# Split weights moved 16 bytes into their buffers in a two-layer hybrid decoder trunk

## The chip, the core and the metric

The kernel runs on one NeuronCore of one Trainium2 chip. Its time is device microseconds from start to end of one execution; the time before is the median of 3 runs. TensorE (PE in the rows) multiplies, PEld is its loading of weights, VectorE is DVE, ScalarE is ACT, GpSimd is POOL, and SyncE (SP) issues most DMAs. SBUF is the memory on the chip, 128 partitions of bytes; an address below is a byte offset within a partition. PSUM is where TensorE accumulates.

## What is computed

Two layers over 512 tokens of width 1024, in float32. Each layer is an input projection that feeds four groups of heads (forgetting attention, gated linear attention, latent attention, state-space scan), an output projection, and a gated feed-forward part of width 2816:

```
h = rmsnorm(x, norm1[l])
(fq, fk, fv, ff, gq, ..., sz, sxbc, sdt) = split_cols(h @ w_in[l], IN_SPLITS)
y_a, y_b, y_c, y_d = fox(...), gla(...), mla(...), mamba2(...)
x = x + concatenate([y_a, y_b, y_c, y_d], axis=-1) @ w_out[l]
h2 = rmsnorm(x, norm2[l])
x = x + (silu(h2 @ w_gate[l]) * (h2 @ w_up[l])) @ w_down[l]
...
return rmsnorm(x, final_norm)
```

## The kernel before

Activations lie with features on the partitions and the 512 tokens along them, as tiles of 128 x 512 float32 (2048 bytes a partition). Every large product is done in float32r, a format with fewer bits that TensorE multiplies in one pass, and float32's accuracy is won back by splitting: each operand is a high part (rounded to float32r) and a low part (what the rounding left). One product of 128 features is therefore three matmuls, in `prod` (lines 315 to 317): high weights by high activations, low weights by high activations, high weights by low activations. Each matmul has a weight load of 128 x 128 ahead of it, then streams 512 tokens. `prod_tok` (lines 324 to 326) has the roles exchanged: 128 tokens of an activation are loaded, and 256 columns of a weight are streamed. Attention scores, transposes and the small products of the scans are plain float32 matmuls, except the forgetting attention's scores (line 692).

Weights come in 204 units of at most 128 x 1024. The class `Weights` holds them: `load` (line 282) issues a DMA into one of two raw buffers `wr`; `split` makes the high part `wh` on ACT (line 293) and the low part `wl` on DVE (line 294), each in one of three buffers; `get` hands out the next unit and keeps two ahead. One unit serves 24 matmuls of 512 columns in the gate, up and front products, and 21 or 24 in the down products.

Order of the work: the front of a layer (normalised activations `n_0h`, `n_0l`, products named `ft`, `sm`, `fkp`, `fqp`, `mckv`, `mcq`, `gq`, `gk`), the heads, whose generators a `Runner` steps between the projections, the output products (`oa`, `og`, `om`), and then the feed-forward part in three pieces of 8, 7 and 7 hidden blocks: for each block a gate product `g` and an up product `u` (activations from the pool `act`), an activation, and the split of the result into `uh` and `ul` (pool `mix`); after each piece eight down products `d` (`dl` in the last piece, whose last two output blocks go in halves of 256 tokens).

Where things lie. Each pool is a run of SBUF addresses, in the order in which the pools are made: constants, residual, `act` (normalised activations), `weights`, `small`, `mix`. The first tile of `small` is a pad of `PAD` float32 that nothing uses; it moves all of `small` and `mix`. In the built program of before:

| buffers | first address | modulo 64 |
|---|---|---|
| `act`: high parts, low parts | 30432, 46816 | 32, 32 |
| `wr` | 63200 | 32 |
| `wh`, `wl` | 71392, 83680 | 32, 32 |
| `uh`, `ul` and all else in `mix` | from 104672 | 32 |

Tiles are multiples of 64 bytes long and blocks start at multiples of 512 bytes, so every float32r product of lines 315 to 326 has both operands at 32 modulo 64: they lie at 0 from each other. The exceptions are constants (`ident`, `ones`, `sel`: 0).

`joint_gates` (line 419 on) computes the gates of two head groups in small tiles of 128 x 32 on DVE; each of its values has a tile of its own.

Of the kernel before, what the change touches and what calls it, by code (L numbers as in the profile page):

```python
# [19 lines left out]
F32R = mybir.dt.float32r  # L20
# [3 lines left out]
P = 128  # L24
# [14 lines left out]
RAWS, PARTS = 2, 3  # L39
# [2 lines left out]
WARM = 14  # L42
ROPE_AT = 3
SECOND_HALF = 4
PAD = 72


FIRST = """N0 A0 P00 N1 A1 P10 P01 P11 N2 P02 P12 B0 N3 P03 P13 B1 N4 P04 P14 N5 P05 P15 N6 P06 P16 N7 P07 P17 W2 Q0 Q1 Q2 Q3
# [87 lines left out]
def trunk(tc, I, out, shapes, depth=2):  # L136
# [3 lines left out]
    def blk(i, n=P):  # L140
        return slice(i * n, (i + 1) * n)

    from contextlib import ExitStack
    with ExitStack() as es:
# [4 lines left out]
        wp = pool("weights", bufs=3)  # L149
        sp = pool("small", bufs=1)  # L150
        mp = pool("mix", bufs=1)

        sp.tile([P, PAD], F32, tag="pad", name="pad")
        pj = pool("psum_proj", bufs=2, space=PSUM)
# [6 lines left out]
        def ps_mix(name):  # L161
            return pm.tile([P, T], F32, tag="pm", name=name)
# [4 lines left out]
        def tmp(tag, name, cols=T, dt=F32, parts=P):  # L167
            return mp.tile([parts, cols], dt, tag=tag, bufs=RINGS[tag], name=name)
# [74 lines left out]
        cs = cp.tile([P, T], F32, name="cs")  # L243
# [26 lines left out]
        class Weights:  # L270
# [14 lines left out]
            def split(self, pieces=1):  # L285

                if not self.loaded:
                    list(self.load())
                raw, i, nk, ncol = self.loaded.pop(0)
                n = nk * ncol  # L290
                h, lo = (wp.tile([P, 1024], F32R, tag=f"w{c}", bufs=PARTS, name=f"w{c}{i}") for c in "hl")
                for c in (blk(j, n // pieces) for j in range(pieces)):
                    S.copy(h[:, c], raw[:, c])  # L293
                    V.tensor_tensor(lo[:, c], raw[:, c], h.bitcast(F32)[:, c], op=ALU.subtract)  # L294
                    yield h, lo
                self.ready.append(tuple(t[:, :n].rearrange("p (k c) -> p k c", k=nk) for t in (h, lo)))
# [55 lines left out]
        class Norm:  # L352
# [43 lines left out]
            def first_two(self, pa_, pb_, split=KC - 1, with_col=True):  # L396

                wa, wb = W.get(), W.get()
                for ks in (range(split), range(split, KC)):
                    for ps, w in ((pa_, wa), (pb_, wb)):  # L400
                        last = prod(ps, w, self.act, ks=ks)
                with tc.issue_after(last.ins):
                    if with_col:
                        self.columns()
                        return self.spread()
                    ps = ps_mix(f"{self.name}ms")
                    PE.matmul(ps, lhsT=ones, rhs=self.acc, start=True, stop=True)
                    return rsqrt(ps, D, "f", self.name, sp.tile([P, T], F32, tag="rn", name=f"{self.name}r"))
# [13 lines left out]
        def joint_gates(l, sm, res):  # L422

            ps = ps_mix(f"jg{l}")
            for b in range(NB):
                PE.transpose(ps[:, 8 * b:8 * b + 8], sm[0:8, blk(b)], ident[0:8, 0:8])
            j = lambda nm: sp.tile([P, 4, 8], F32, tag=f"j{nm}", name=f"j{nm}{l}")
            f2 = lambda t: t.rearrange("p b c -> p (b c)")
            bcast = lambda t: t.unsqueeze(1).broadcast_to((P, 4, 8))
            y, e, s, s2, p, spl, a, csum, tot = (j(n) for n in ("y", "e", "s", "q", "p", "sp", "a", "cs", "tot"))  # L430
            V.tensor_tensor(y, ps[:, 0:32].rearrange("p (b c) -> p b c", b=4), bcast(gsgn), op=ALU.mult)
            V.tensor_tensor(y, y, bcast(gbias[:, l, :]), op=ALU.add)
            V.scalar_tensor_tensor(e, y, -1.0, y, op0=ALU.mult, op1=ALU.max)
            S.activation(e, e, AF.Exp, scale=-1.0)

            V.tensor_scalar(s, e, 2.0, None, op0=ALU.add)
            V.reciprocal(s, s)
            V.tensor_tensor(s, e, s, op=ALU.mult)
            V.tensor_tensor(s2, s, s, op=ALU.mult)
            V.tensor_scalar(p, s2, 2.0 / 17, None, op0=ALU.mult)  # L440
            for k in range(7, 0, -1):
                V.scalar_tensor_tensor(p, p, 2.0 / (2 * k + 1), s2, op0=ALU.add, op1=ALU.mult)
            V.scalar_tensor_tensor(p, p, 2.0, s, op0=ALU.add, op1=ALU.mult)
            V.scalar_tensor_tensor(spl, y, 0.0, p, op0=ALU.max, op1=ALU.add)
            V.tensor_tensor(a, spl, bcast(gfac[:, l, :]), op=ALU.mult)
            yield
            pc_ = ps_mix(f"jc{l}")
            PE.matmul(pc_[:, 0:32], lhsT=tri, rhs=f2(a), start=True, stop=True)
            PE.matmul(pc_[:, 32:64], lhsT=ones, rhs=f2(a), start=True, stop=True)
            V.tensor_copy(f2(csum), pc_[:, 0:32])  # L450
            V.tensor_copy(f2(tot), pc_[:, 32:64])

            pre = sp.tile([P, 3, 4], F32, tag="jpre", name=f"jpre{l}")
            V.tensor_copy(pre[:, 0, :], tot[:, 0, 0:4])
            for b in (1, 2):
                V.tensor_tensor(pre[:, b, :], pre[:, b - 1, :], tot[:, b, 0:4], op=ALU.add)
            V.tensor_tensor(csum[:, 1:4, 0:4], csum[:, 1:4, 0:4], pre, op=ALU.add)
            yield
            pr = ps_mix(f"jr{l}")
            for b in range(NB):  # L460
                PE.transpose(pr[0:8, blk(b)], csum[:, b, :], ident)
            rows = sm[0:8]
            S.copy(rows, pr[0:8, :])
            rr = sp.tile([40, T], F32R, tag="jrr", name=f"jrr{l}")
            G.memset(rr.bitcast(F32), 0.0)
            V.tensor_copy(rr[0:8], rows)
            V.tensor_tensor(rr[32:40], rows, rr.bitcast(F32)[0:8], op=ALU.subtract)

            ncs = sp.tile([P, 4, 4], F32, tag="jn", name=f"jn{l}")
            V.tensor_scalar(ncs, csum[:, :, 4:8], -1.0, None, op0=ALU.mult)  # L470
            dec = sp.tile([P, 4, 4], F32, tag="jd", name=f"jd{l}")
            V.tensor_tensor(dec, ncs, tot[:, :, 4:8], op=ALU.add)
            res.update(rr=rr, spl=spl, ncs=ncs, dec=dec, tot=tot)
# [414 lines left out]
        for l in range(depth):  # L888
# [8 lines left out]
            V.tensor_tensor(sm, ps, r, op=ALU.mult)  # L897
            gates = {}
            R.start(joint_gates(l, sm, gates))


            rg, fr = [], []
            for j in range(10):
# [5 lines left out]
                a = tmp("f", f"fa{l}_{j}")  # L909
# [5 lines left out]
                else:  # L915
                    c = tmp("f", f"cv{l}_{j}")
# [52 lines left out]
            for c in range(2):  # L969
                hold = {}  # L970
                for nm, scale, one, row in (("k", 1.0, -1.0, 66), ("q", -0.125, 1.0, 64)):
                    ps = ps_proj(f"f{nm}p{l}_{c}")
                    prod(ps, W.get(), act)
                    for hh in range(2):
                        h, sl = 2 * c + hh, blk(hh, 64)
                        t = tmp("f", f"f{nm}t{l}_{h}", parts=64)
                        a, b = (tmp("cb"[c], f"f{nm}{i}{l}_{h}", dt=F32R, parts=n) for i, n in (("a", P), ("b", 68)))
                        V.scalar_tensor_tensor(t, ps[sl], scale, r[sl], op0=ALU.mult, op1=ALU.mult)
                        S.copy(a[0:64], t)
                        lo, again = (b[0:64], a[64:128]) if nm == "k" else (a[64:128], b[0:64])  # L980
# [72 lines left out]
            for i in range(4):  # L1053
                w = W.get()
# [8 lines left out]
            for nm, ops in (("g", mix_g), ("m", mix_m)):  # L1063
                if nm == "m":
                    R.drain(g_m)
                for i in range(2):
                    w = W.get()
# [15 lines left out]
            for j0, j1 in HID_PARTS:  # L1083
                us = []
                for j in range(j0, j1):
# [5 lines left out]
                    t, s = tmp("f", f"ft{l}_{j}"), tmp("f", f"fs{l}_{j}")  # L1091
# [48 lines left out]
```

## Time and profile before

| | |
|---|---|
| median of 3 runs | 1269.92 us (1268.7 to 1270.27) |
| profiled execution | 1269.87 us |
| its span, first to last instruction | 1268.1 us |
| granted TensorE clock, mean | 0.994 |
| PE busy | 1248.9 us (98%) |
| DVE busy, ACT busy | 694.0 us (55%), 533.5 us (42%) |

A matmul's end is modelled in this profile, and one matmul's record runs on into the next one's, so TensorE's pace is read from the starts of matmuls that follow one another, not from their durations. In rows of single instructions the first column is the start in microseconds, the second the duration. A granted clock of 1.00 is TensorE's level of 2.4 GHz, 0.50 the level of 1.2 GHz.

### The profile page before, as it was taken

How to read it: one execution, taken by the hardware profiler on the slowest of the kernel's cores; microseconds unless marked ns; L12 is line 12 of the kernel's file. 1: busy time of each engine (PE TensorE's matmuls, PEld its weight loads, DVE VectorE, ACT ScalarE, POOL GpSimd, SP SyncE). 2: the span in 40 equal slices, each digit the busy share in tenths (PEclk: the TensorE clock that was granted, in tenths of full speed). 3: DMA queues.
4: the chain of work that ended last, by engine and by line, in shares of the span. 5: the costliest groups of instructions: out<-in, count | busy, mean ns of one | idle time of the engine just before them, and what ended most of it. 6: DMA issues, size and time to landing. Idle time of an engine off the chain costs nothing.

```text
span 1268.1 us, 16210 instructions
## 1 busy us (share of the span) xinstructions
PE 1248.9 (98%) x6402; PEld 1014.5 (80%) x6402; DVE 694.0 (55%) x1132; ACT 533.5 (42%) x882; POOL 179.1 (14%) x163
## 2 busy tenths in 40 slices
PE   9999999989999999999999999999899999999997
PEld 7887787768888888888888877777788888888886
DVE  7877697565443333344557677966644334433444
ACT  6557765543222222223444577565422222212232
POOL 0103210031100110111301122000211011101111
PEclk9999999989999999999999999999999999999999
DMA  6222121113333333332323221212233223333232
GB/s 206 89 84 67 58 68 45 47 60 116 90 95 99 100 94 91 103 96 89 110 83 101 84 67 43 67 34 67 68 116 97 89 96 100 89 109 98 88 89 76
DMA packets 32907, 109.99 MB, mean 87 GB/s; under 512 B 4096, under 2 KB 4256, under 8 KB 32832
## 3 DMA queue, kind: packets, MB, share of 16 engines
q1 hardware_dynamic: 31968, 108.54, 27.7%
q8 instruction: 50, 0.82, 0.3%
q10 hardware_dynamic: 288, 0.34, 0.1%
q14 instruction: 25, 0.20, 0.0%
q0 software_dynamic: 576, 0.08, 0.0%
HBM read 106.79 MB, written 2.10 MB: 86 GB/s over the span
## 4 chain that ended last, share of the span: by engine, by line
PE 92%; DVE 5%; ACT 2%; DMA 1%; issue 0%; POOL 0%; SPq 0%; DVEq 0%
PE u L315 6%; PE u L316 6%; PE u L317 6%; PE g L317 6%; PE g L315 6%; PE g L316 6%; PE d L315 5%; PE d L316 5%; PE d L317 5%; PE ft L317 3%; PE ft L316 3%; PE ft L315 3%; PE sm L692 1%; PE oa L316 1%; PE oa L315 1%; PE oa L317 1%
## 5 line engine op out<-in xcount | busy, mean ns | idle before, releaser
L293 ACT CAST wh<-wr 128x1024 fp32r<-128x1024 f32 (+2 forms) x206 | 210.3, 1023 | 567.1 <-issue 342.5
L294 DVE TENSOR_TENSOR wl<-wr,wh 128x1024 fp32r<-128x1024 f32 (+2 forms) x206 | 249.9, 1213 | 73.2 <-ACT wh L293 73.0
L315 PE MATMUL d<-uh,wh 128*128 128x512 f32 x296 | 115.1, 389 | 0.0
L316 PE MATMUL d<-uh,wl 128*128 128x512 f32 x296 | 115.1, 389 | 0.0
L317 PE MATMUL d<-ul,wh 128*128 128x512 f32 x296 | 115.1, 389 | 0.0
L1097 DVE TENSOR_TENSOR ft<-u,fs 128x512 f32<-128x512 f32 x44 | 30.4, 692 | 132.7 <-PE u L317 127.1
L1111 DVE TENSOR_TENSOR xT<-xT,d 128x512 f32<-128x512 f32 x40 | 27.5, 688 | 104.6 <-PE d L317 104.6
L1094 POOL TENSOR_TENSOR fs<-fs,n_0r 128x512 f32<-128x512 f32 x22 | 38.3, 1744 | 280.4 <-ACT fs L1093 280.4
L1094 POOL TENSOR_TENSOR fs<-fs,n_1r 128x512 f32<-128x512 f32 x22 | 38.3, 1745 | 279.3 <-ACT fs L1093 279.3
L317 PE MATMUL g<-n_1l,wh 128*128 128x512 f32 x176 | 69.0, 392 | 2.3 <-DVE n_1l L364 2.3
L317 PE MATMUL g<-n_0l,wh 128*128 128x512 f32 x176 | 69.0, 392 | 2.3 <-DVE n_0l L364 2.3
L315 PE MATMUL g<-n_0h,wh 128*128 128x512 f32 x176 | 69.0, 392 | 0.8 <-ACT n_0h L363 0.8
L315 PE MATMUL g<-n_1h,wh 128*128 128x512 f32 x176 | 69.0, 392 | 0.8 <-ACT n_1h L363 0.8
L315 PE MATMUL u<-n_0h,wh 128*128 128x512 f32 x176 | 69.5, 395 | 0.0
L316 PE MATMUL u<-n_0h,wl 128*128 128x512 f32 x176 | 69.4, 394 | 0.0
L317 PE MATMUL u<-n_0l,wh 128*128 128x512 f32 x176 | 69.4, 394 | 0.0
L315 PE MATMUL u<-n_1h,wh 128*128 128x512 f32 x176 | 69.0, 392 | 0.0
L317 PE MATMUL u<-n_1l,wh 128*128 128x512 f32 x176 | 69.0, 392 | 0.0
L316 PE MATMUL u<-n_1h,wl 128*128 128x512 f32 x176 | 68.9, 392 | 0.0
L316 PE MATMUL g<-n_0h,wl 128*128 128x512 f32 x176 | 68.5, 389 | 0.0
L316 PE MATMUL g<-n_1h,wl 128*128 128x512 f32 x176 | 68.5, 389 | 0.0
L317 PEld LDWEIGHTS d<-ul,wh 128*128 128x128 f32 x296 | 55.6, 188 | 11.6
(614 smaller groups left out, 2823.5 us busy)
## 6 DMA issues: line engine op xcount, KB each, us to landing
wr<-in_weights_dram SPq DMA_DIRECT2D x168, 512.0 KB, 3.5
wr<-in_weights_dram SPq DMA_DIRECT2D x32, 448.0 KB, 3.2
xT<-in_x_dram SPq DMA_DIRECT2D x8, 256.0 KB, 6.8
out_dram<-foo SPq DMA_DIRECT2D x8, 256.0 KB, 2.4
wr<-in_weights_dram SPq DMA_DIRECT2D x6, 256.0 KB, 4.1
posi<-in_positions_dram ACTq DMA_DIRECT2D x1, 256.0 KB, 3.0
fkb<-jrr POOLq DMA_DIRECT2D x8, 4.0 KB, 2.7
fqb<-jrr POOLq DMA_DIRECT2D x8, 4.0 KB, 1.7
```

The lines of the kernel that those rows point to most:

```text
L293: S.copy(h[:, c], raw[:, c])
L294: V.tensor_tensor(lo[:, c], raw[:, c], h.bitcast(F32)[:, c], op=ALU.subtract)
L315: PE.matmul(ps, lhsT=wh[:, k, c0:c0 + P], rhs=ah, start=k == 0, stop=False)
L316: PE.matmul(ps, lhsT=wl[:, k, c0:c0 + P], rhs=ah, start=False, stop=False)
L317: last = PE.matmul(ps, lhsT=wh[:, k, c0:c0 + P], rhs=al, start=False, stop=k == n - 1)
L692: PE.matmul(ps[:, :n], lhsT=q[:d, blk(qb)], rhs=k[:d, :n], start=i == 0, stop=i == len(terms[h]) - 1)
L1094: G.tensor_tensor(s, s, r, op=ALU.mult)
L1097: V.tensor_tensor(t, pu, s, op=ALU.mult)
L1111: V.tensor_tensor(xT[m], xT[m], ps, op=ALU.add)
```

## The change

`wh` and `wl` get 1040 columns in place of 1024 (4160 bytes a partition), and what is used of them begins at column 4, 16 bytes in. To make room, `PAD` goes from 72 to 16, and in `joint_gates` the values `a` and `csum` take over the tiles of `e` and `s`, which have been read for the last time by then. In the built program the split weights then lie at 48 modulo 64 (first used byte 71408), `act` stays at 32, and `uh`, `ul` and the rest of `mix` move to 0. Modulo 64 bytes the operands of the gate, up and front products lie at 48 from the weights (32 - 48), and those of the down products at 16 (0 - 48). Output products of the heads and of the latents read one kind or the other: `oa`, `og`, `om` operands are in `act`, the latents' in `mix`. No instruction is added, removed or moved on any engine; the waits are the same ones, and the tile names `ja` and `jcs` are gone.

```diff
-PAD = 72
+PAD = 16
...
-                h, lo = (wp.tile([P, 1024], F32R, tag=f"w{c}", bufs=PARTS, name=f"w{c}{i}") for c in "hl")
+
+                h, lo = (wp.tile([P, 1040], F32R, tag=f"w{c}", bufs=PARTS, name=f"w{c}{i}")[:, 4:1028] for c in "hl")
                 for c in (blk(j, n // pieces) for j in range(pieces)):
                     S.copy(h[:, c], raw[:, c])
                     V.tensor_tensor(lo[:, c], raw[:, c], h.bitcast(F32)[:, c], op=ALU.subtract)
...
-            y, e, s, s2, p, spl, a, csum, tot = (j(n) for n in ("y", "e", "s", "q", "p", "sp", "a", "cs", "tot"))
+            y, e, s, s2, p, spl, tot = (j(n) for n in ("y", "e", "s", "q", "p", "sp", "tot"))
+            a, csum = e, s
```

## Rows read from the trace of the kernel before

**Rows 1.** The page: engines' busy time, share of span, instructions; then the chain by engine.
```profile
PE 1248.9 (98%) x6402; PEld 1014.5 (80%) x6402; DVE 694.0 (55%) x1132; ACT 533.5 (42%) x882; POOL 179.1 (14%) x163
...
PE 92%; DVE 5%; ACT 2%; DMA 1%; issue 0%; POOL 0%; SPq 0%; DVEq 0%
```

**Rows 2.** Busy time by stretch: a warming stretch, then feed-forward parts of both layers.
```profile
core 0: us, PE busy (x) PEld busy (x) DVE busy (x) ACT busy (x) POOL busy (x), PEclk, DMA share, GB/s
273.00:283.00 10.00, 8.84 (x27) 7.06 (x28) 2.37 (x3) 0.26 (x2) 0.56 (x1) 0.66 0.18 54
300.00:360.00 60.00, 60.00 (x267) 49.67 (x266) 24.11 (x27) 17.37 (x22) 10.81 (x6) 1.00 0.32 102
1000.00:1060.00 60.00, 60.00 (x266) 49.69 (x265) 22.35 (x25) 14.36 (x17) 5.40 (x3) 1.00 0.30 97
```

**Rows 3.** Timeline, down products of layer 1: matmuls and the loads beside them.
```profile
999.72 0.39 PE L317 MATMUL d<-ul,wh 128*128 128x512 f32 x1
999.95 0.39 PE L315 MATMUL d<-uh,wh 128*128 128x512 f32 x1
999.95 0.19 PEld L316 LDWEIGHTS d<-uh,wl 128*128 128x128 f32 x1
1000.17 0.39 PE L316 MATMUL d<-uh,wl 128*128 128x512 f32 x1
1000.18 0.19 PEld L317 LDWEIGHTS d<-ul,wh 128*128 128x128 f32 x1
...
1011.96 0.39 PE L317 MATMUL d<-ul,wh 128*128 128x512 f32 x1
```

**Rows 4.** Timeline, token products of layer 0, 256 columns: first and last of 38.
```profile
86.83 0.28 PE L325 MATMUL fvp<-wl,n_0h 128*128 128x256 f32 x1
...
91.27 0.28 PE L326 MATMUL fvp<-wh,n_0l 128*128 128x256 f32 x1
```

**Rows 5.** Timeline: plain float32 scores of 512 columns, and what follows them.
```profile
216.63 1.88 PE L692 MATMUL sm<-mkh,mqh 128*128 128x512 f32 x4
218.34 0.60 PE L709 MATMUL ptm<-ident,asm 128*128 128x128 f32 x4
```

**Rows 6.** Timeline, up products at the lower clock: first and last of nine.
```profile
275.18 0.63 PE L316 MATMUL u<-n_0h,wl 128*128 128x512 f32 x1
...
278.59 0.63 PE L315 MATMUL u<-n_0h,wh 128*128 128x512 f32 x1
```

**Rows 7.** Timeline, output products just after small products of the attention: second of nine on.
```profile
220.93 0.40 PE L316 MATMUL oa<-ms_1mh,wl 128*128 128x512 f32 x1
221.16 0.40 PE L317 MATMUL oa<-ms_1ml,wh 128*128 128x512 f32 x1
...
222.55 0.40 PE L317 MATMUL oa<-f_1ml,wh 128*128 128x512 f32 x1
222.79 0.61 PE L692 MATMUL sm<-mkh,mqh 128*128 128x128 f32 x4
```

**Rows 8.** By tile, durations min/median/max: down products, then some output products.
```profile
L315 PE MATMUL d<-uh,wh x296: 389/389/389, 360.4 to 1140.0; 128*128 128x512 f32 x148
...
L316 PE MATMUL oa<-f_0mh,wl x16: 387/396/504, 195.7 to 860.8; 128*128 128x512 f32 x16
```

**Rows 9.** By line over the span (PE, PEld): line 315, line 324; then `dl`'s shapes.
```profile
0.00:1268.10 1268.10, 605.84 (x1538) 290.01 (x1538) 0.99 0.28 87
...
0.00:1268.10 1268.10, 39.60 (x136) 25.99 (x136) 0.99 0.28 87
...
L315 PE MATMUL dl<-uh,wh x70: 277/389/481, 1216.9 to 1258.4; 128*128 128x512 f32 x42, 128*128 128x256 f32 x28
```

**Rows 10.** Groups by shape: splits of whole units on DVE and ACT; busy, mean, idle before.
```profile
L294 DVE TENSOR_TENSOR wl<-wr,wh 128x1024 fp32r<-128x1024 f32 x168 | 210.8, 1255 | 65.0 <-ACT wh L293 64.8
L293 ACT CAST wh<-wr 128x1024 fp32r<-128x1024 f32 x168 | 176.3, 1052 | 452.6 <-issue 259.2 <-PE d L317 83.7 <-PE g L317 46.0
```

**Rows 11.** By tile: `joint_gates`' `ja`, the value that takes over the tile of `e`.
```profile
L445 DVE TENSOR_TENSOR ja<-jsp,gfac x2: 181/187/193, 38.9 to 660.5; 128x32 f32<-128x32 f32 x2
```

## The prediction

> **What bounds the kernel now.** I read the page first, for who is busy and what the end hangs on: TensorE is busy 98% of the span and makes up 92% of the chain that ended last, DVE 5% [rows 1]. Then the busy time by stretch: in the feed-forward parts TensorE has no idle time at a granted clock of 1.00, the 2.4 GHz level, while DVE is busy 22 to 24 us of 60, ACT 14 to 17, and the DMA share is 0.30 to 0.32 [rows 2]. So no wait is to be looked for; the kernel goes as fast as matmul follows matmul. The third view is the timeline, of which the reader takes starts alone. From 999.72 to 1011.96 us there are 54 gaps between down products, 12.24 / 54 = 226.7 ns each [rows 3]. At 2.4 GHz that is 544 cycles for 512 columns: 32 cycles, 13.3 ns, more than one column a cycle. The token products have 37 gaps in 4.44 us, 120.0 ns or 288 cycles for 256 columns [rows 4]: 32 over again. The excess goes with each load and matmul, not with the columns.
>
> Where does it not appear? Plain float32 scores take 1.71 us for four passes of 512 columns, 427.5 ns each, against 426.7 for a column every second cycle: 0.8 ns over, with the same kind of load beside each [rows 5]. And while the clock stood at its lower level (granted 0.66 on average over that stretch) the same float32r products had 8 gaps in 3.41 us, 426.3 ns, which is 512 columns at 1.2 GHz and nothing over [rows 2, 6]. A fixed price for changing weights would show there too. The load of the next weights begins with the stream, within 10 ns [rows 3], so I read the 13.3 ns as the two disturbing each other in SBUF when the stream takes a column every cycle. The last view says that this depends on how the two lie to each other: right after small products the same shape runs from 220.93 to 222.79 us in 8 gaps, 232.5 ns each [rows 7], and over the run the modelled records of output products have a median of 396 ns and a smallest of 387, where all 296 down products of one line have 389 [rows 8]. In an undisturbed stream it settles at one value.
>
> **The change part by part.** The same instructions stand in the same order. What changes is where loads and streams begin within 64 bytes. Before, they begin 0 apart, in the same 16 bytes; after, one quarter of 64 bytes apart in one direction (48) or the other (16).
>
> 1. The products. 1538 matmuls on each of lines 315 to 317 and 136 on each of 324 to 326 [rows 9]: 3 x 1538 + 3 x 136 = 5022 that load one of the split pair and stream the other. The trace has no products at 16 or 48, so the price per product is bounded from both sides. Best: the excess shrinks to that of the float32 passes, 13.3 - 0.8 = 12.5 ns less, 5022 x 12.5 = 62.8 us. Worst: the gap stays at what the disturbed records show, 396 against 389 ns, 7 ns more, or 35 us. The smallest record, 387, would be 2 ns less, or 10 us. I take half of the excess, 6.7 ns (16 cycles), 5022 x 6.7 = 33.5 us less. It is nearer to the float32 end than to the smallest record, because every row that I have is at offset 0, where both begin in the same place, and that is the one arrangement that the change leaves; and because the settled excess is the same whole 32 cycles in two shapes, I expect another step of the same kind, not a few cycles. The part of the products that run at the lower clock is too small to take off.
>
> A rule of the Trainium skill goes against this: "TensorE: Matmul & The Clock Gate", Step-by-step: what each phase is for, says that TensorE reads SBUF for the stream and for the loads through two independent ports, so that the next load takes nothing from the running matmul. By that rule there would be nothing to win, and the sum would be 0. The same page, Back-to-back issue gap, gives N / 2.4 + 2.5 ns for a single stream, 215.8 ns for 512 columns; this trace disagrees by 10.9 ns a product [rows 3], and if that were the gap after, my estimate from the page would be 1215 us.
>
> 2. The splits. ACT and DVE now write 16 bytes into the buffer, 1052 and 1255 ns for a whole unit [rows 10]. The cover in the feed-forward part is an engine with over half of its time free [rows 2]. Without cover, DVE's 5% of the chain is 63 us [rows 1]; if all of it were 5% slower or faster, 3 us either way. I take 0. Faster products ask for a unit every 24 x 220 = 5.3 us where it was 5.4; one split of 1.3 us and one cast of 1.1 fit.
>
> 3. `mix` moves to 0 modulo 64. The attention's own matmuls have both operands in `mix`, which stay 0 apart; constants (`ident`, `ones`) now lie with them where they were 32 away. 6402 - 5022 = 1380 matmul records are left [rows 1, 9]; most are short float32 passes, which have shown 0.8 ns of excess [rows 5]. At that size 1 us either way; I take 0.
>
> 4. `a` and `csum` in the tiles of `e` and `s`: written by DVE after DVE's own last reading of them, two instructions of 187 ns a layer [rows 11], with no new engine to wait for. In layer 1 `e` is written 600 us after layer 0's last reader. 0, and at worst 2 x 0.2 us.
>
> Sum, against the profiled execution: 1269.87 - 33.5 = 1236.4 us. Its span is 1268.1 with 1.8 us around it; the median of the runs differs by 0.05 us, so the same number stands for the median.
>
> **The rivals.**
>
> *No change.* The 32 cycles are the price of changing weights in a one-pass product, or collisions whose number does not depend on where the two begin. For it: 32 cycles for both widths, and a settled gap that holds to the nanosecond through whatever DVE and ACT do [rows 3, 4, 8]. Against it: nothing over at the lower clock, and the wide spread when disturbed [rows 6, 7]. 1269.9, within 2 us.
>
> *Slower: offset 0 is a good place.* The settled gap before lies near the short end of what the disturbed records show (387 to 396 and more). If at 16 and 48 the streams settle where disturbed ones now run, 232.5 ns, each product pays 5.8 ns more: 5022 x 5.8 = 29 us, 1299; by the median record of 396, 1305. It decides as soon as the gap after is over 226.7 ns in the feed-forward part, since no idle time there can take it up [rows 2].
>
> *All of the excess goes.* 1269.9 - 62.8 = 1207. For it the float32 passes [rows 5]; against it, that no disturbed record falls below 387.
>
> *48 and 16 are not alike.* Leaving the few latent products aside, down products are 3 x 296 + 3 x 70 = 1098 of the 5022 [rows 8, 9]; 1098 x 6.7 = 7.3 us, the others 26.2. With opposite signs the sum is 19 us to one side or the other: 1251 or 1289.
>
> **How the numbers follow.** Half of the excess goes: 0.36, with its own range 1222 to 1260 (from three quarters of the excess to the 2 ns of the smallest record). All of it: 0.13. Opposite signs: 0.10, of which 0.06 faster. No change: 0.14. Slower: 0.27. Faster by over 0.2% (2.5 us, about what a measurement here can tell from nothing) is 0.36 + 0.13 + 0.06 = 0.55; the same 0.14; slower 0.27 + 0.04 = 0.31. The range, 1210 to 1296 us, takes in the forecast, no change, both mixed cases, half of the case in which all goes, and two thirds of the slower one: about 0.84.
>
> **What would show it right or wrong.** Right: in the timeline of the down, gate and up products the gap is near 220 ns, and that of the token products near 113; DVE's and ACT's durations are as before; TensorE stays fully busy in the feed-forward parts. The first step is wrong if the gap is 226.7 as before (no change) or above it (slower), and its size is wrong if it is some other value under 226.7. The rival of unlike offsets shows as different gaps for `d` and for `g`, `u`, `ft`. Idle time of TensorE ahead of `wh` or `wl` would show step 2 wrong.

## The result, and the profile after

The changed kernel is slower: 1287.51 us, median of 4 runs (1287.03 to 1287.85), against 1269.31 (1268.07 to 1270.27) for the kernel before on the same chip. The ratio is 1.0144, with a 95% interval of 1.0126 to 1.0161. The forecast was 1236.4; the time lies in the range of 1210 to 1296.

The page of the changed kernel, engines' busy time first (share of the span of 1286.1 us, instructions), then the two groups of splits by shape:

```profile
PE 1266.8 (99%) x6402; PEld 1013.9 (79%) x6402; DVE 693.8 (54%) x1132; ACT 532.7 (41%) x882; POOL 178.9 (14%) x163
```

```profile
L295 DVE TENSOR_TENSOR wl<-wr,wh 128x1024 fp32r<-128x1024 f32 x168 | 210.9, 1256 | 63.5 <-ACT wh L294 63.4
L294 ACT CAST wh<-wr 128x1024 fp32r<-128x1024 f32 x168 | 175.5, 1047 | 468.5 <-issue 276.3 <-PE d L318 85.9 <-PE g L318 43.7
```

Every engine but TensorE does what it did, to the microsecond [rows 1]: 1256 and 1047 ns a split against 1255 and 1052 [rows 10]. TensorE alone is 17.9 us longer with the same 6402 matmuls. The busy time by stretch says that no wait was added. Columns: engine busy time and instructions in the stretch, granted clock, DMA share, GB/s.

```profile
300.00:360.00 60.00, 60.00 (x260) 48.62 (x259) 23.82 (x27) 17.35 (x22) 9.37 (x6) 1.00 0.31 97
1000.00:1060.00 60.00, 60.00 (x261) 48.72 (x260) 21.67 (x23) 13.12 (x14) 3.32 (x2) 1.00 0.30 93
```

TensorE is still full, at a granted clock of 1.00, but it passes 260 and 261 matmuls in 60 us where it passed 267 and 266 [rows 2]. So each one is longer. The timeline shows it, first for down products of layer 1, first and last of 54, then for gate and up products, first and last of 51, then for token products of 256 columns, first and last of the 47 behind the first.

```profile
999.67 0.39 PE L316 MATMUL d<-uh,wh 128*128 128x512 f32 x1
...
1011.92 0.39 PE L318 MATMUL d<-ul,wh 128*128 128x512 f32 x1
```

```profile
300.15 0.39 PE L317 MATMUL g<-n_0h,wl 128*128 128x512 f32 x1
...
311.80 0.40 PE L316 MATMUL g<-n_0h,wh 128*128 128x512 f32 x1
```

```profile
86.58 0.28 PE L326 MATMUL fvp<-wl,n_0h 128*128 128x256 f32 x1
...
91.99 0.28 PE L327 MATMUL fvp<-wh,n_0l 128*128 128x256 f32 x1
```

The gap of the down products is 12.25 / 53 = 231.1 ns, where it was 226.7 [rows 3]; that of gate and up products 11.65 / 50 = 233.0 here, with a median of 232 over all of them. Token products go at 5.41 / 46 = 117.6 ns, a little faster than 120.0 [rows 4]. The old gap was even; the new one wanders between 0.22 and 0.24 us from one product to the next and never settles. Added up over all starts: 2112 gate and up products cost 10.9 us more, 888 down products 3.9, 480 front products (`ft`) 2.9. These three make 17.7 of the 18.0 us by which the span grew. The other 1542 products of split weights cost 1.4 us more together, 0.9 ns each: most of those between small products had no settled gap to lose [rows 7]. The time between all remaining matmuls fell by 1.1 us.

### The profile page after: what moved, and what is told of

The parts are those of the page before. It is cut to its first block, busy times and chain, and to the rows that moved or that the text cites. A ratio compares the mean times of both kernels' runs of the same rounds, so it can differ in the third digit from the quotient of the medians.

```text
span 1286.1 us, 16210 instructions
## 1 busy us (share of the span) xinstructions
PE 1266.8 (99%) x6402; PEld 1013.9 (79%) x6402; DVE 693.8 (54%) x1132; ACT 532.7 (41%) x882; POOL 178.9 (14%) x163
## 4 chain that ended last, share of the span: by engine, by line
PE 92%; DVE 5%; ACT 2%; issue 1%; DMA 0%; POOL 0%; SPq 0%; DVEq 0%
PE u L318 6%; PE u L317 6%; PE u L316 6%; PE g L318 6%; PE g L317 6%; PE g L316 6%; PE d L317 5%; PE d L318 5%; PE d L316 5%; PE ft L317 3%; PE ft L318 3%; PE ft L316 3%; PE sm L694 1%; PE oa L317 1%; PE oa L316 1%; PE oa L318 1%
```

## The experiments

One number is needed for all of them, the **distance**: first byte of the weights less first byte of the streamed operand, modulo 256. Why 256, experiment 3 shows. Experiments 1 and 2 were planned with 64 in mind. The **gap** is the time from one product's start to the next one's; a stretch settles when the gap no longer drifts but repeats, and its settled gap is the mean over the last 40 or so.

**1. A short program of products alone, offsets in steps of 4 bytes.**

```diff
+            for n, (name, cols, o, p) in enumerate(plan()):
...
+                for i in range(N_EACH):
+                    k = o + P * (i % 12)
+                    PE.matmul(ps[:, 0:cols], lhsT=wt[:, k:k + P], rhs=act[:, p:p + cols], start=i == 0,
+                              stop=i == N_EACH - 1)
```

> Nothing of the reference is computed: 54 stretches of 72 float32r products each, one core, nothing else running; two plain float32 products between stretches. sxa to sxp: stream of 512 columns at 32 modulo 64, weights from 0 in steps of 4 bytes up to 60; sya to syp: the same with the stream at 0; sz: stream and weights moved together; sh: as sx with 256 columns. Theory 1 (the place of the stream against the weights modulo 64 decides whether the gap settles): sxi (weights at 32, 0 apart) settles at 226.7 ns, sxm (weights at 48, 48 apart) and sym (stream 0, weights 48, 16 apart) do not settle and stand at 230 to 233 ns on average; sx and sy show the same pattern, shifted by 32 bytes, and every sz at a multiple of 16 bytes is at 226.7. Theory 2 (where the weights start, by themselves): sx and sy alike without a shift, sz at 48 as slow as sxm. Theory 3 (something else in the kernel, not the products): all 54 at 226.7 or 120.

Rows of the timeline for a settled part of a stretch hold 41 products each: start, time from first start to modelled end, name. The last product's own 0.39 us comes off, and the rest is 40 gaps. Here: weights and stream moved together by 16 bytes (`sze`), by 0 (`sya`), and apart (`sxb`).

```profile
583.49 9.45 PE L104 MATMUL sze<-act,wt 128*128 128x512 f32 x41
...
291.07 9.55 PE L104 MATMUL sya<-act,wt 128*128 128x512 f32 x41
...
32.86 9.89 PE L104 MATMUL sxb<-act,wt 128*128 128x512 f32 x41
```

226.5, 229.0 and 237.5 ns. No stretch of 512 columns is below 226.7 (by the starts of single records, which have more digits); of 38 only two settle there, the rest lie between 228 and 240. Not even the arrangements meant as the kernel's own are at 226.7: `sya`, both operands at 0, and `sxi`, both at 32, give 228.9. So more than the place modulo 64 decides: both have their operands 64 apart modulo 512, the kernel before 0.

**2. The change taken apart.** Its 16 bytes taken out, with its longer buffers kept (`no16`); `mix` at 32 as before, with the 16 bytes kept (`at48_48`); the shared gate tiles and another absolute place alone (`all_at_0`).

```diff
 no16 against after
-PAD = 16
+PAD = 24
-... wp.tile([P, 1040], ...)[:, 4:1028] ...
+... wp.tile([P, 1040], ...)[:, 0:1024] ...
 at48_48 against after
-PAD = 16
+PAD = 24
 all_at_0 against before
+ap.tile([P, 8], F32, tag="lead", bufs=1, name="lead")
-y, e, s, s2, p, spl, a, csum, tot = ...
+y, e, s, s2, p, spl, tot = ...
+a, csum = e, s
```

> The changed kernel with its longer buffers, its shared gate tiles and a pad, but the split weights start at byte 0 of their buffers and the pad is 24, so that both kinds of operands are 0 from the weights again. Theories 1 and 2 (the 16 bytes): as before, 1269 within 2 us. Theory 3 (the shared tiles, or the longer buffers): as after, 1287.

> The changed kernel with a pad of 24 in place of 16: the down products' operands go from 16 to 48 from the weights, and all of mix from 0 to 32 modulo 64; gate, up and front products stay at 48. Theory 1: gate, up and front products as after (232 ns); down products go from 231 to those products' 232, and the time from 1287.5 to 1288 or 1289. If mix at 0 modulo 64 is what costs: 1280 or less.

> The kernel before with 32 bytes of pad ahead of the activations and the shared gate tiles: weights, activations and mix all at 0 modulo 64 in place of 32, 0 from each other as before. Theory 1 (place against each other): 226.7 ns and 1269 within 2 us. Theory 2 (absolute place): another gap, either shorter, since every operand now starts on 64 bytes, or longer, and a time off by 10 us or more.

`no16` took 1284.29 us (ratio 1.0122, 1.0107 to 1.0137), `at48_48` 1288.49 (1.0152, 1.0135 to 1.0169), `all_at_0` 1269.25 (1.0001, 0.9992 to 1.0010). So neither the gate tiles nor the place of `mix` matters, and the surprise is `no16`: without any offset, buffers of 4160 bytes cost 15 us. Both of the theories on 64 bytes fall with it. What is left: six buffers of 4160 bytes, one behind the other, no longer begin at one place. In the built programs the high weights of the kernel before begin 0 from the stream modulo 512 in all buffers; in `no16` the three high buffers lie at 0, 64 and 128 and the low ones at 192, 0 and 64 modulo 256 for gate and up products, each 64 further for down products. Its down products, first and last of 52, run at 11.78 / 51 = 231.0 ns:

```profile
1000.12 0.39 PE L317 MATMUL d<-uh,wl 128*128 128x512 f32 x1
...
1011.90 0.39 PE L317 MATMUL d<-uh,wl 128*128 128x512 f32 x1
```

**3. Distances: a second short program, and the whole kernel at 64 and at 192.** The short program has 104 stretches, not the 95 that its expectation counts. In the whole kernel a tile of 64 or of 192 bytes ahead of the weight buffers moves them all alike.

```diff
 lead64 (lead192: 48 columns, and PAD = 24) against before
+wp.tile([P, 16], F32, tag="lead", bufs=1, name="lead")
-PAD = 72
+PAD = 56
```

> Left out: the whole network; 64 products in float32r stand one behind the other in each of 95 stretches, 512 columns wide (256 in ha, hb, hc, hd), every operand from one long tile whose first byte is 0 modulo 512. Turns as in the kernel: weights one, weights two, weights one. da, db, dc, dd: weights 0, 16, 32, 224 bytes into a 512-byte line, the streamed operand 0, 64, ... 448 further on. de, df, dg: the steps of 16 between. mx: only the second weights are moved by that much; my: only the third product's stream. no and np: the distances of the three buffers in the kernel with 4160-byte buffers read from their start (gate and up, down). Theory 4 (the gap settles at 226.7 ns only where the stream and the weights stand 0 apart modulo 128 or 256, and the longer buffers broke that): dd000, dd128 or at least dd256 at 226.7, dd064 and dd192 at 229 to 233; no000 to no002 and np000 to np002 at 229 to 233. Theory 5 (no distance matters as such, but the products that follow each other must all have the same one): all dd, da, dc at 226.7, and mx, my, no, np at 229 to 233 wherever the moved operand differs. Theory 2 (where the weights begin absolutely): rows of da, db, dc, dd differ from each other as groups, not along themselves.

> The kernel before with buffers of 1024 and a tile of 64 bytes ahead of all weight buffers (and 64 bytes less behind them): both weights of every unit stand 64 bytes on from the streamed activations modulo 512, for gate, up, front and down products alike; nothing else changes. Theory 4: as slow as with longer buffers, 1282 to 1290, the gap of the down products 230 to 232 ns. Theory 5: all products alike, so 1269 and 226.7 ns.

> As lead64, but the tile ahead of the weight buffers is 192 bytes: every stream stands 64 on from its weights modulo 256, where the short program showed 228.9 ns. Theory 4: gap of the down products 228.9, a third of the way from 226.7 to lead64's 233.3, and a time a third of the way from 1269.1 to 1293.2: 1277. If what counts is only settled or not, 1285 to 1293.

The settled part of `dd` in the short program, the stream 0, 64, 128, 192 and 256 bytes on from the weights (distances 0, 192, 128, 64 and 0 again), in this order:

```profile
65.32 9.46 PE L128 MATMUL dd<-big 128*128 128x512 f32 x41
...
125.53 9.55 PE L128 MATMUL dd<-big 128*128 128x512 f32 x41
...
186.78 9.72 PE L128 MATMUL dd<-big 128*128 128x512 f32 x41
...
247.87 9.73 PE L128 MATMUL dd<-big 128*128 128x512 f32 x41
...
308.26 9.46 PE L128 MATMUL dd<-big 128*128 128x512 f32 x41
```

With 0.39 off and through 40: 226.8, 229.0, 233.2, 233.5, 226.8 ns. The rows 320 to 448 repeat 64 to 192 to within 0.1 ns: the period is 256 bytes, and at 32-byte places only distance 0 settles at 226.7. `mx`, in which the low weights alone are moved, gives 231.1 at 64, 128 and 192: one operand out of place is enough. Theory 5 falls with `dd`, where all products are alike.

The whole kernel gives the same numbers. Down products, `lead64` (distance 64), first and last of 52, then `lead192`, first and last of 53:

```profile
1000.05 0.39 PE L316 MATMUL d<-uh,wh 128*128 128x512 f32 x1
...
1011.95 0.40 PE L316 MATMUL d<-uh,wh 128*128 128x512 f32 x1
```

```profile
1000.10 0.39 PE L317 MATMUL d<-uh,wl 128*128 128x512 f32 x1
...
1012.00 0.39 PE L318 MATMUL d<-ul,wh 128*128 128x512 f32 x1
```

11.90 / 51 = 233.3 and 11.90 / 52 = 228.8 ns, as in the short program (233.3 and 228.9). The times are 1293.22 us (1.0193, 1.0176 to 1.0210) and 1275.88 (1.0049, 1.0032 to 1.0065; 1277 was expected). `lead64` missed its expected 1282 to 1290 by 3 us: the expectation was taken from `no16`, and a uniform 64 is worse than a mixture.

**4. The 16 bytes by themselves, first reading.** A third short program takes the changed kernel's own places; in the whole kernel (`downs`) each of 32 down products gets another offset inside a buffer of the old length.

```diff
+if (nk, ncol) == (7, P):
+    o = SHIFTS[self.seven] // 4
+    self.seven += 1
+    h, lo = h[:, o:o + n], lo[:, o:o + n]
```

> Left out: the whole network; 64 float32r products in each stretch as in distances, 512 columns unless named. ag: gate weights and stream where the changed kernel has them, for its three buffers in turn; ad: the same for its down products. ae: both weights 0, 16, ... 240 bytes on from the stream. wp, wq, wr, ws: stream 0, 64, 128, 192 bytes on from the weights, with weights 128, then 64, then 32 columns wide. ta: 256 columns, stream 192 on, weights at 16, 80, 144, 208. tb: 512 columns, stream 64 on. xa, xb, xc: weights at 0, 4, ... 28 with the stream 0, 64, 192 on. co: 128, 256, 384, 512 columns at distance 0. Theory 4, now with a period of 256 bytes and a part for the absolute place: ag and ad 229 to 234, like the changed kernel's 232 and 231; aea 226.7; the 16 bytes alone (aeb) 229 to 234 or, were they harmless, 226.7; xa settled only at 0, xb and xc only at 16; tb all 226.7; ta all 113. If the excess over 512 columns at full clock (213.3) is the weight load's reading beside the stream, wp falls from 226.7 to about 220 with 64 columns of weights and 217 with 32, and the rows wq to ws draw together with it; if it belongs to the stream alone, the width of the weights changes nothing.

> The kernel before, where the weights of each down product with seven chunks (32 of the 48, whose units leave 512 bytes of their buffer empty) begin 0, 16, ... 240 bytes into the buffer, another offset for each product: layer 0 takes all sixteen in order, layer 1 takes 240, 192, 16, 128, 64, 0, 176, 32, 64, 128, 192, 16 again. Buffers keep their 4096 bytes. Theory 4: the gap is read product by product: 226.7 ns at 0, near 228.9 at 192 (stream 64 on), 233.3 at 128 and at 64; the 16 bytes by themselves 229 to 234. In the whole about 2 us more than before, 1270 to 1273. Were a mixture of lengths or neighbours the cause, all stay at 226.7, since high and low weights always stand alike.

Gate and down arrangements of the changed kernel gave 230 to 233 ns in the short program (`ag`, `ad`), as in the kernel. The 16 bytes alone (`aeb`) settled at 226.7. In `downs` (one run, 1271.21 us) the first products of layer 0's second part begin 0, 16 and 32 bytes in; rows: first and last of 20 records at 16, then of 21 at 32.

```profile
483.71 0.39 PE L320 MATMUL d<-uh,wh 128*128 128x512 f32 x1
...
488.02 0.39 PE L321 MATMUL d<-uh,wl 128*128 128x512 f32 x1
488.48 0.39 PE L320 MATMUL d<-uh,wh 128*128 128x512 f32 x1
...
493.14 0.39 PE L322 MATMUL d<-ul,wh 128*128 128x512 f32 x1
```

4.31 / 19 = 226.8 and 4.66 / 20 = 233.0. Over the last twelve gaps of each of the 24 products `d`: 226.7 at 0, 16 and 144; 228.9 at 192; 229.9 at 176; 231.7 to 234.4 at all others but 240, which gave 228.3 in layer 0 and 226.7 in layer 1. I read from this that 16 bytes are harmless. That was wrong, and two hints were in the trace: the two values at 240, and a product that I did not read. Of the eight products `dl` at the end of layer 1 one begins 16 bytes in (1233.26 to 1238.28 us); two small matmuls interrupt it, and behind them it goes at 233.3. One distance, two gaps.

The width of the weights missed its expectation: with 64 and with 32 columns of weights `wp` went to 230.0 and 231.7 instead of down. So the excess is not simply the time that the load reads. One more missed: `xc` settled nowhere at 226.7. With both operands at 16 and the distance 64 it gave 228.9 (`xce`), where `db` had given 226.7 at the same places modulo 256.

**5. The 16 bytes by themselves, in all units.** First as slices of one long tile (`ring0` without, `alone16` with 16 bytes). In both, some units share a slice while both are in use, so some products read other weights than the reference's.

```diff
-PAD = 72
+PAD = 64
+self.ring = wp.tile([P, 6 * 1024 + 8], F32R, tag="ring", bufs=1, name="ring")
-h, lo = (wp.tile([P, 1024], ...) for c in "hl")
+o = 0 + 1024 * (i % PARTS)       # alone16: 4 + ...
+h, lo = self.ring[:, o:o + 1024], self.ring[:, o + 3072:o + 4096]
```

> The control for alone16: the six split buffers are slices of 4096 bytes in one long tile, that begins where the first buffer began, so that weights of every unit lie 0 from the stream modulo 256, as before. The scheduler moves some instructions in the front part of each layer. All theories: the gap of the down, gate and up products 226.7 ns, and within 0.3% of before (1266 to 1273).

> As ring0 with the same order of instructions, but each of the six slices begins 16 bytes later: the change's 16 bytes in every unit, without its longer buffers. Theory 4 with the table of the short programs (16 off modulo 256 settles, and so it did in the down products of downs): gap 226.7 ns in gate, up and down, time within 0.2% of ring0. Theory 2 (the 16 bytes cost what the change costs): gap 229 to 234, 1280 to 1290.

`ring0` missed: 1282.99 us (1.0109, 1.0095 to 1.0123), though its gaps are those of before (226.7). From first to last product its feed-forward parts take 365 and 327 us, against 366 and 327 before; the time is lost ahead of them, 5 us in layer 0 and 9 in layer 1, where the instructions have another order. So only its gaps are used. `alone16` took 1285.7 in the profiled execution and 1303.6 to 1307.8 in the six others, all at a granted clock of 0.990 to 0.993. The trace, output products `om` (first and last of 42) and then up and gate products (first and last of 50):

```profile
262.20 0.40 PE L319 MATMUL om<-m_0ml,ring 128*128 128x512 f32 x1
...
271.77 0.40 PE L318 MATMUL om<-m_0mh,ring 128*128 128x512 f32 x1
...
300.26 0.39 PE L317 MATMUL u<-n_0h,ring 128*128 128x512 f32 x1
...
311.37 0.39 PE L318 MATMUL u<-n_0h,ring 128*128 128x512 f32 x1
```

9.57 / 41 = 233.4 and 11.11 / 49 = 226.7 ns, at one and the same distance in one trace. Its last down products show the step from one to the other: first and last of 27 before an interruption by two small matmuls, then first and last of 20 behind it.

```profile
1232.49 0.39 PE L317 MATMUL dl<-uh,ring 128*128 128x512 f32 x1
...
1238.39 0.39 PE L319 MATMUL dl<-ul,ring 128*128 128x512 f32 x1
1238.72 0.44 PE L779 MATMUL fo<-ident,xg 128*128 128x128 f32 x2
...
1239.23 0.40 PE L318 MATMUL dl<-uh,ring 128*128 128x512 f32 x1
...
1243.67 0.39 PE L319 MATMUL dl<-ul,ring 128*128 128x512 f32 x1
```

5.90 / 26 = 226.9 before and 4.44 / 19 = 233.7 behind. In `ring0`, with the same instructions at distance 0, the gap is back at 226.7 within eleven products of each such interruption. Hence the question of the last three runs: two rhythms? `len4352` and `len4352_16` keep the order of before and have buffers of 17 x 256 bytes.

```diff
-h, lo = (wp.tile([P, 1024], F32R, ...) for c in "hl")
+h, lo = (wp.tile([P, 1088], F32R, ...)[:, 0:1024] for c in "hl")     # len4352_16: [:, 4:1028]
-nc = bacc.Bacc(..., dynamic_dma_scratch_size=4096)
+nc = bacc.Bacc(..., dynamic_dma_scratch_size=2048)
```

> The kernel before with split buffers of 4352 bytes (17 times 256) where the change has 4160, and nothing in the added 256 bytes; the instructions stand in the order of before. (Room is made in a scratch area of 2 KB that nothing here fills.) Weights of every unit stay 0 from the stream modulo 256. Theory 4: 1269, within 0.2% of before, gap 226.7; were longer buffers as such the cause: 1284, as with 4160.

> As len4352, with the weights 16 bytes into each buffer, in all units: the 16 bytes by themselves, in the order of before. Two readings of what was seen at distance 16. (a) It settles at 226.7, as in pairs and downs: 1269 to 1272, all runs alike. (b) At distance 16 the products have two rhythms, 226.7 and 233.3, and a disturbance decides in which they go on (in alone16 the gate, up and down products ran in the first, the front products in the second, and single runs lay 18 to 22 us above the profiled one): runs that scatter between 1273 and 1294, the gap 226.7 in some products and 233 in others of one trace.

> Left out: the whole network. 64 products of 512 columns in a stretch as in pairs, but the second, third and fourth product of each stretch have 64, 92, ... 484 columns (letters a to p), so that the rhythm begins in sixteen ways. Weights 0 (ka), 16 (kb), 240 (kc), 144 (kd), 192 (ke) bytes on from the stream. If the distance alone decides, a group has one gap whatever its start: ka, kb, kc 226.7, ke 228.9. If some distances have two rhythms, ka is 226.7 in all sixteen, and kb, kc or kd show 226.7 in some and 230 to 234 in others.

`len4352`: 1269.43 us (1.0002, 0.9993 to 1.0010). Longer buffers cost nothing at this length, a multiple of 256. `len4352_16`: 1290.53 us (1.0174, 1.0160 to 1.0188), all five runs between 1289.9 and 1292; the scatter that reading (b) expected did not come. So the 16 bytes by themselves cost 21 us. Its trace, output products `og` (first and last of 21), then up and gate products (first and last of 49):

```profile
248.00 0.39 PE L317 MATMUL og<-mg_0ml,wh 128*128 128x512 f32 x1
...
252.53 0.39 PE L316 MATMUL og<-mg_1mh,wl 128*128 128x512 f32 x1
...
300.22 0.39 PE L315 MATMUL u<-n_0h,wh 128*128 128x512 f32 x1
...
311.42 0.39 PE L315 MATMUL u<-n_0h,wh 128*128 128x512 f32 x1
```

4.53 / 20 = 226.5 and 11.20 / 48 = 233.3: again both in one trace, and here the feed-forward parts, in which products follow each other without a pause, were entered in the slow rhythm and stayed in it. In the short program `starts` the rows are distance 0 (`kaa`) and distance 16 after two different beginnings (`kba`, `kbb`):

```profile
19.53 9.46 PE L103 MATMUL kaa<-big 128*128 128x512 f32 x41
...
255.52 9.73 PE L103 MATMUL kba<-big 128*128 128x512 f32 x41
...
270.41 9.46 PE L103 MATMUL kbb<-big 128*128 128x512 f32 x41
```

226.8, 233.5 and 226.8. All sixteen beginnings:

```
distance    settled gap, ns (how many of 16 beginnings)
0           226.7 (16)
16          226.7 (3)    233.3 (13)
144         226.7 (3)    233.3 (13)
192         228.9 (14)   233.3 (2)
240         226.7 (10)   228.4 (6)
```

## Why the prediction was wrong

**Step 1, the products, failed.** It took 6.7 ns off each of 5022 products. The trace after shows more, not less: on the mean 5.2 ns a product for `g` and `u`, 4.4 for `d` and 6.0 for `ft`, 3480 products in all, and 0.9 ns for the others. The sign hung on one argument: the nearest rows were those of the float32 passes, since all float32r rows stood "at offset 0", which the change leaves. The argument fails twice.

- Offset 0 was not one arrangement among equals. Of the five distances of `starts` it is the only one that came back to 226.7 from all sixteen beginnings, and no float32r stretch of 512 columns went below 226.7. The excess of 13.3 ns is what is left at best, not what the old places cost. That it held "to the nanosecond" [rows 3, 8], which I counted for "no change", was no sign either way: at distance 64 the short program holds 233 to 234 ns just as evenly (`dd`, fourth row).
- The change was described modulo 64, by its first bytes alone. The period is 256, and a buffer of 4160 bytes moves the next one by 64. The weights of one product lie at 16 and 208 from the stream in one buffer, at 80 and 16 in the next, at 144 and 80 in the third (gate and up). "48" and "16" never described the products.

The price falls into two parts, each enough by itself: the length alone 15 us (`no16`), the 16 bytes alone 21 us (`len4352_16`), both 18. They do not add, since either ends the settled gap, and a mixture (231.1 to 233) is no worse than the slow rhythm (233.3).

**The rival "offset 0 is a good place" happened**, with the gap it named: disturbed products showed 232.5 ns [rows 7], and the feed-forward part now runs at 231 to 233. That the figure fits so well is in part luck: it is the mean over several distances that a buffer length of 4160 mixes, and the rival knew of two. That the time lies in the stated range is owed to this rival, not to the forecast. Its 1299 was 11.5 us too high, because it let all 5022 products pay. The 256-column ones went the other way (117.6 for 120.0), and those between small products had been disturbed before. It had 0.27; by the rows it deserved more than the forecast, as the disturbed products were the only float32r rows of another state, and their gaps (232.5) and their median record (396) lay on its side.

**The weighed rule.** The Trainium skill, "TensorE: Matmul & The Clock Gate", Step-by-step: what each phase is for, has stream and loads read through two independent ports, so that a load takes nothing from the running matmul. The kernel's traces disagree: the same products with the weights 64 bytes elsewhere go from 226.7 to 233.3 ns (`lead64`). That there was nothing to win came true, but the sum of 0 that the prediction drew from the rule did not: the change cost 18 us.

**Steps 2 to 4 held.** The splits kept their durations; `all_at_0` shows that shared gate tiles cost nothing, and `at48_48` that the place of `mix` did not help (1288.49, 1 us above the changed kernel). TensorE had no new idle time. Of the marks that would show step 1 right, 220 ns and 113 ns, neither came.

**What stays open.** Which reading meets which at distance 0, and why a constant 32 cycles remain there; and why `alone16` entered its feed-forward parts in the fast rhythm once. No trace of its slower executions exists, so that they ran at 233 is inferred: from `len4352_16`, and because 3000 products `g`, `u` and `d` at 6.7 ns more would be 20 us, where those executions took 18 to 22 us more.

## What to carry to other kernels

Where single-pass products follow each other without a pause, look at the starts, not the durations, and compare the gap with that of another placement: its size tells, not its evenness, since here 233.3 ns came back after every disturbance too (`lead64`). Keep weight and stream buffers at one place modulo 256 bytes, and that a multiple of 32 (16 bytes off one, `db` gave 230.0 at distance 0), and check the length of every rotating buffer as well as its first byte; a length like 4160 spreads them. A placement that looks settled in a short test may have a second rhythm, so start it in several ways, or time it in the whole kernel, before believing it.

## What the runs showed of the hardware

- Float32r products with a new load each time: 111.7, 120.0, 173.3 and 226.7 ns for 128, 256, 384 and 512 columns at distance 0 (`co`). From 256 on, 128 columns more cost 53.3 ns, one column a cycle at 2.4 GHz, plus a constant 13.3 ns.
- The gap depends on where weights and stream lie to each other, with a period of 256 bytes: 226.7, 233.3, 233.3, 228.9 ns at 0, 64, 128 and 192 for weights at a 32-byte place. With both operands 16 bytes off such a place distance 192 settles at 226.7 (`db`, `tb`); the two programs differ at 64 (226.7 in `db`, 228.9 in `xce`) and at 0 (230.0 and, in `xae`, 233.3).
- For 256 columns the order is another: 120.0 ns at distance 0, 117.8 at 64 and 192 (`ha`), and 113.3 at distance 64 with both operands 16 off (`ta`, stream 192 on). In this kernel that would be worth at most 408 x 6.7 = 2.7 us, if all other products stayed settled; it wasn't tried, since the activations would have to move as well.
- One distance can have two stable rhythms. A stream keeps the one it entered for hundreds of microseconds (226.7 ns from 293 to 638 us in `alone16`), and an interruption by two small matmuls can move it to the other (233.3).
